# Output projection of a hybrid diffusion layer: rounded tokens kept over both column halves, the two contraction halves in PSUM tiles of their own, squares summed by column half

## The chip, the cores and the metric

The kernel runs on one core of a Trainium2 chip. The metric is the device time of one execution in microseconds (us). Five engines work beside each other, each in its own program order: TensorE (PE; its weight loads are listed as PEld), VectorE (DVE), ScalarE (ACT), GpSimd (POOL) and SyncE (SP, which issues most DMAs). They wait for each other through semaphores.

## The reference, cut to what matters

One layer over 128 context tokens and 512 latent tokens, model width 1024. Attention and a gated convolution each give 512 columns per token; each half is RMS-normed on its own, both together go through one output projection, and a feed-forward block follows.

```
merged = concat([_rms(attn, attn_out_norm), _rms(y_conv, conv_out_norm)], axis=-1)   # 512 + 512
mix = merged @ w_out                                  # (tokens, 1024) @ (1024, 1024)
x  = x + g1 * mix
h2 = _rms(x, norm_ffn) * (1 + sc2) + sh2              # the mean of squares runs over all 1024 columns
gate, up = split(h2 @ w_gate_up)                      # DFF = 2816
x  = x + g2 * ((silu(gate) * up) @ w_down)
```

`_rms(v, g) = v * rsqrt(mean(v*v) + 1e-6) * g`. The inverse norms of the two halves, `rA` (attention) and `rB` (convolution), are numbers per token, so they can be applied after the matmul, to the product of each half.

## The kernel before, in words

Every float32 operand is split into a rounded part and a rest (`split`, L146: ACT writes the high part, DVE subtracts to get the low part), and a product is three matmuls (`mm3`, L150: high x high, high x low, low x high).

The output projection is the loop at L1037. It runs over two column halves `j` of `w_out` (512 columns each) and, in each, over five tiles of 128 tokens: the context tile first, then latent tiles 0 to 3 (`TORD`). For each tile the tokens are the stationary operand: four 128-row blocks of the attention half `of` and four of the convolution half `yf`. Both halves are split anew in each `j` (`mix_half`, L968), except for the attention half of the context tile, which was split earlier (`mix_ctx`). The products of the halves go to the two banks of one PSUM tile `ab`; 24 matmuls per tile. Then ACT writes `m = ab[1]*rB`, DVE adds `ab[0]*rA`, multiplies by the gate `g1`, and adds `m` to the residual `x2` (L1071 to L1075; GpSimd does the last two steps for the first two tiles of `j = 0`). In `j = 1` ACT squares all 1024 columns of `x2` with a sum (L1080), DVE scales it, GpSimd takes the power -1/2, and DVE writes the normed tile `x2n` (L1082). `h2_turn` transposes a tile's `x2n` on TensorE, always after the 24 matmuls of the next tile of `j = 1`.

The weights of the projection come in eight blocks `("o", j, kp)` of two 128-row chunks, through three buffers `wf`; ACT (L244) writes the high part `wh` and DVE (L245) the low part `wl` with the norm gains folded in. Beside that, in `j = 0`, DVE accumulates the second gate in `aacc` (`g2_step`, L986 and L988, from four loads that go through the same three buffers).

Behind the projection the normed tokens are put, as high and low parts, into quarters: `B11`, `B21` for token columns 0 to 319 (LO), `B12`, `B22` for 320 to 639 (HI); `B12` is a buffer of the tag `gT`. Four differences `T1` to `T4` of the quarters follow (`b_sums`; its scratch is `tr`). The first two feed-forward blocks, f = 0 and 1 (`plain`, L1102), multiply by the quarters, first LO of both, then HI of both, 48 matmuls each. From f = 2 on, seven products by sums and differences of weight blocks are used (`op_load`: `S1` to `S4` are built in `sx`), in the order A11, S1, S2, A12, S3, A22, S4; S2 accumulates in the PSUM tile of A11, so it waits until ACT has copied that tile to `p1` (L1129).

TensorE's order is written out by hand (`manual_schedule` for PE, L467). On DVE, ACT, GpSimd and SP a scheduler puts the program into a fixed order at build time, after priorities that `early(n)` raises; at run time every engine keeps to that order. `BHD` names the quarters whose high part DVE writes instead of ACT.

Of the kernel before, what the change touches and what calls it, by code (L numbers as in the profile page):

```python
# [9 lines left out]
F32 = mybir.dt.float32  # L10
F32R = mybir.dt.float32r
AF = mybir.ActivationFunctionType
ALU = mybir.AluOpType
AX = mybir.AxisListType

P = 128
D = 1024
KD = D // P
NL = 4
NT = 5  # L20
TOK = NT * P
CTX = 4
# [8 lines left out]
EPS = 1e-6  # L31
# [30 lines left out]
H2E = [0, 0, 0, 2, 0]  # L62
PX = 2
SPO = 0
BHD = ("B21", "B22")
TL = 1
G2N = 0
PT = 2
# [1 line left out]
PHB = 2  # L70
XP = [50, 400]
BP = 300
AWB = 2
AO = 6
SOON = 150
# [12 lines left out]
def build(ctx, tc, x_prompt, x_sample, c, cache_k, cache_v, c_ctx, norm_mix, norm_ffn, w_ada, b_ada,  # L88
# [3 lines left out]
    act, dve, pool, pe, sp = nc.scalar, nc.vector, nc.gpsimd, nc.tensor, nc.sync  # L92
# [4 lines left out]
    def open_pool(name, side, names):  # L97
        g = tc.tile_pool(name=name, bufs=1, side=side, reuse_waits="tile")
        pools[name] = (g, g.__enter__())
        for n in names.split():  # L100
            where[n] = name

    def open_psum(name, bufs):
        g = tc.tile_pool(name=name, bufs=1, space=bass.MemoryType.PSUM, reuse_waits="tile")
        pools["psum"] = (g, g.__enter__())
        pbufs.clear()
        pbufs.update(bufs)
# [8 lines left out]
    def T(tag, shape, dt=F32, bufs=1):  # L116
        seq[0] += 1
        return pools[where.get(tag, "A")][1].tile(list(shape), dt, tag=tag, bufs=bufs, name=f"{tag}_{seq[0]}")
# [15 lines left out]
    def PS2():  # L134
        return PB((P, 2, 512), tag="s")
# [7 lines left out]
    def early(n):  # L143
        return tc.high_priority(n)

    def split(hi, lo, src):  # L146
        act.activation(hi, src, AF.Copy)  # L147
        dve.tensor_tensor(lo, src, f32(hi), ALU.subtract)  # L148

    def mm3(out, lh, ll, rh, rl, start, stop, more=False):  # L150
        pe.matmul(out, lh, rh, start=start, stop=False, skip_group_check=more)  # L151
        pe.matmul(out, lh, rl, start=False, stop=False, skip_group_check=more)  # L152
        pe.matmul(out, ll, rh, start=False, stop=stop, skip_group_check=more)  # L153
# [141 lines left out]
    for gi, grp in enumerate(GROUPS):  # L295
# [5 lines left out]
        for j in range(2):  # L301
            for i0 in range(0, len(grp), 2):
                n = len(grp[i0:i0 + 2])
# [450 lines left out]
    rB = [None] * NT  # L754
# [176 lines left out]
    close_pool("B1")  # L931
    close_pool("H")
    close_pool("psum")
    open_psum("pp3", {"t": 2, "c": 2, "s": 2})
    for x in PPO:
        for _ in range(1):
            kept[x] = [PS2() if x == "s" else PB(tag=x)]
    open_pool("X", "left", "x2 x2n g2 sx")
    open_pool("GT", "left", "gT")
    open_pool("Y1", "left", "B11 B21")  # L940
    open_pool("D", "right", "mix mH mL aacc bb")
    phase[0] = 2


# [20 lines left out]
                else:  # L965
                    act.activation(dst, tp[:, i], AF.Identity, bias=b, scale=a)

    def mix_half(src):  # L968
        mh = T("mH", (P, 4, P), F32R, 4)
        ml = T("mL", (P, 4, P), F32R, 4)  # L970
        split(mh, ml, src)
        return mh, ml

    g2 = [T("g2", (P, D), F32, 2) for _ in range(2)]
    g2acc = [None, None]
# [61 lines left out]
    for j in range(2):  # L1037
        cols = slice(j * 512, (j + 1) * 512)
        for n, t in enumerate(TORD):
            cc = 1 if t == CTX else 0  # L1040
            c0 = t * P + (2 if t == CTX else 0)
            ms = [mix_ctx if t == CTX else mix_half(of[t]), mix_half(yf[:, :, c0:c0 + P])]
            ab = PS2()
            for half in range(2):
                for p in range(4):
                    wh, wl = W(("o", j, 2 * half + p // 2))
                    mm3(ab[:, half], ms[half][0][:, p], ms[half][1][:, p], wh[:, p % 2], wl[:, p % 2],
                        p == 0, p == 3)
                if j == 0 and CRP == f"{n}{'me'[half]}":
                    next(ada_gen, None)  # L1050
                    conv_rms()
            if j == 1 and n:
                h2_turn(TORD[n - 1])
                with early(BP):
                    if n == 2:
                        b_plain("B11 B21", slice(0, 256))
                    if n == 3:
                        b_plain("B11 B21", slice(256, HALF))
            if j == 0 and n == 1:
                att_rms(NL - 1)  # L1060
                act.activation(warm, rA[NL - 1], AF.Silu)
            if j == 0 and G2N <= n < 4 + G2N:
                g2_step(0, n - G2N)
            if j == 1 and n == 0:
                g2_out(0)
            if j == 0:
                x2[t] = T("x2", (P, D), F32, NT)
                sp.dma_start(x2[t], x_dram[t])
            with early(XP[j]):
                m = T("mix", (P, 512), F32, 2)  # L1070
                act.activation(m, ab[:, 1], AF.Copy, scale=rB[t])  # L1071
                dve.scalar_tensor_tensor(m, ab[:, 0], rA[t], m, ALU.mult, ALU.add)
                e = pool if j == 0 and n < PX else dve
                e.tensor_tensor(m, m, g1[cc][:, cols], ALU.mult)
                e.tensor_tensor(x2[t][:, cols], m, x2[t][:, cols], ALU.add)  # L1075
            if j == 1:
                with early(XP[j]):
                    x2n[t] = T("x2n", (P, D), F32, 1)
                    ss = T("ss", (P, 1), F32, 6)
                    act.activation(x2n[t], x2[t], AF.Square, accum_out=ss)  # L1080
                    r = rstd_of(ss, 1, 1.0 / D)
                    dve.tensor_scalar_mul(x2n[t], x2[t], r)  # L1082


# [211 lines left out]
```

## Time and profile before

| | |
|---|---|
| median of 3 runs | 761.24 us (761.2 to 762.45) |
| the profiled execution | 762.03 us, of which its span (first to last instruction) is 760.3 us |
| granted TensorE clock, mean | 0.995 |
| DMA | 84.52 MB in 102349 packets, mean 111 GB/s |
| chain that ended last | PE 80%, DVE 9%, ACT 3%, DMA 3% of the span |

All durations further down come from the profiled execution; times are counted from its first instruction. In rows of the timeline the first number is the start, the second the duration, and a bracket at the end names idle time of that engine ahead of the row and what ended it. Consecutive instructions of one engine overlap a little, so the distance of two starts is what one of them costs in a row of many.

### The profile page before, as it was taken

The page shows a single profiled execution, that of the slowest core. Times are in us where ns is not written, and L with a number is a line of the kernel's source. Part 1 is how long each engine was busy: PE and PEld are TensorE (multiplying, and loading weights), DVE is VectorE, ACT ScalarE, POOL GpSimd, SP SyncE. Part 2 cuts the span into 40 slices and gives each one's busy share as a digit, 9 for nine tenths or more (in the row PEclk, how much of TensorE's full clock was granted, in tenths as well). Part 3 has the DMA queues.
Part 4 walks back from the last instruction along what each step waited for, and adds up shares of the span by engine and source line. Part 5 has one row for each costly group of instructions (what it writes and reads, how often), then busy time and mean ns, then how long its engine had stood idle before and what let it go on. Part 6 is the DMA issues. An engine that isn't in the chain of part 4 may idle for free.

```text
span 760.3 us, 11889 instructions
## 1 busy us (share of the span) xinstructions
PE 738.2 (97%) x4580; PEld 663.4 (87%) x4580; DVE 559.1 (74%) x1009; ACT 373.6 (49%) x713; POOL 48.7 (6%) x77
## 2 busy tenths in 40 slices
PE   4999999999999999999999999999999999999997
PEld 3778988989999887799998789998889998899986
DVE  5556987676567799799879678875578866788653
ACT  5355776666555445865552135552125541255410
POOL 2104201011010130000000000000000000000000
PEclk9899999999999999999999999999999999999999
DMA  9994133423423453031325223223113132232312
GB/s 291 289 258 138 43 111 110 155 91 106 159 91 117 156 199 112 1 111 56 112 90 176 85 66 98 81 90 111 52 56 111 57 111 80 60 87 81 112 55 84
DMA packets 102349, 84.52 MB, mean 111 GB/s; under 512 B 4526, under 2 KB 82674, under 8 KB 102292
## 3 DMA queue, kind: packets, MB, share of 16 engines
q1 hardware_dynamic: 100980, 83.39, 36.1%
q8 instruction: 36, 0.59, 0.3%
q10 hardware_dynamic: 1056, 0.26, 0.2%
q14 instruction: 21, 0.17, 0.1%
q0 software_dynamic: 256, 0.11, 0.1%
HBM read 79.68 MB, written 2.75 MB: 108 GB/s over the span
## 4 chain that ended last, share of the span: by engine, by line
PE 80%; DVE 9%; ACT 3%; DMA 3%; issue 2%; SPq 1%; POOL 1%; POOLq 0%; DVEq 0%; ACTq 0%
PE pf L151 17%; PE pf L152 17%; PE pf L153 17%; PE pc L674 3%; PE pc L675 3%; PE pc L676 3%; PE ps L788 2%; PE po L831 2%; PE pt L814 2%; PE ps L151 2%; DMA af<-in_w_ada_dram 2%; PE pc L376 2%; PE ps L152 2%; PE ps L153 2%; POOL rs L161 1%
## 5 line engine op out<-in xcount | busy, mean ns | idle before, releaser
L147 ACT ACTIVATE wh<-wf 128x1024 fp32r<-128x1024 f32 (+1 forms) x76 | 64.2, 844 | 92.7 <-PE pf L153 63.1
L151 PE MATMUL pf<-wh,gT 128*128 128x512 f32 (+1 forms) x225 | 88.1, 391 | 0.0
L152 PE MATMUL pf<-wl,gT 128*128 128x512 f32 (+1 forms) x225 | 87.7, 390 | 0.0
L153 PE MATMUL pf<-wh,gT 128*128 128x512 f32 (+1 forms) x225 | 87.6, 390 | 0.0
L148 DVE TENSOR_TENSOR wl<-wf,wh 128x1024 fp32r<-128x1024 f32 (+1 forms) x42 | 49.3, 1174 | 28.1 <-ACT wh L147 25.2
L674 PE MATMUL pc<-hH,wh 128*128 128x320 f32 x192 | 61.1, 318 | 0.0
L676 PE MATMUL pc<-hH,wl 128*128 128x320 f32 x192 | 59.4, 309 | 0.0
L675 PE MATMUL pc<-hL,wh 128*128 128x320 f32 x192 | 59.3, 309 | 0.0
L151 PEld LDWEIGHTS pf<-wh,gT 128*128 128x128 f32 x225 | 42.2, 188 | 9.9 <-ACT wh L147 0.2
L152 PEld LDWEIGHTS pf<-wl,gT 128*128 128x128 f32 x225 | 42.2, 188 | 9.9 <-issue 0.2
L153 PEld LDWEIGHTS pf<-wh,gT 128*128 128x128 f32 x225 | 42.2, 188 | 9.8
L151 PE MATMUL pf<-T,wh 128*128 128x320 f32 x160 | 49.3, 308 | 1.5 <-ACT p L1129 1.5
L151 PE MATMUL pf<-T,wl 128*128 128x320 f32 x160 | 49.2, 308 | 0.0
L152 PE MATMUL pf<-T,wl 128*128 128x320 f32 x160 | 49.2, 308 | 0.0
L153 PE MATMUL pf<-T,wl 128*128 128x320 f32 x160 | 49.2, 308 | 0.0
L152 PE MATMUL pf<-T,wh 128*128 128x320 f32 x160 | 49.2, 308 | 0.0
L153 PE MATMUL pf<-T,wh 128*128 128x320 f32 x160 | 49.2, 307 | 0.0
L151 PE MATMUL pf<-B,wl 128*128 128x320 f32 x152 | 46.9, 308 | 0.0
L152 PE MATMUL pf<-B,wl 128*128 128x320 f32 x152 | 46.8, 308 | 0.0
L153 PE MATMUL pf<-B,wl 128*128 128x320 f32 x152 | 46.8, 308 | 0.0
L1208 DVE TENSOR_TENSOR dm<-pf,g 128x512 f32<-128x512 f32 (+1 forms) x41 | 27.7, 675 | 23.1 <-PE pf L153 23.1
L147 ACT ACTIVATE wl<-wf 128x512 fp32r<-128x512 f32 x34 | 21.4, 630 | 43.5 <-PE pf L152 36.8
(282 smaller groups left out, 2055.7 us busy)
## 6 DMA issues: line engine op xcount, KB each, us to landing
wf<-in_w_gate_up_dram SPq DMA_DIRECT2D x44, 512.0 KB, 4.0
aw<-in_w_ada_dram SPq DMA_DIRECT2D x24, 512.0 KB, 4.8
wf<-in_w_down_dram SPq DMA_DIRECT2D x20, 512.0 KB, 3.4
wf<-in_w_in_dram SPq DMA_DIRECT2D x18, 512.0 KB, 5.7
af<-in_w_ada_dram SPq DMA_DIRECT2D x32, 256.0 KB, 5.8
x<-in_x_sample_dram SPq DMA_DIRECT2D x8, 512.0 KB, 5.2
wf<-in_w_out_dram SPq DMA_DIRECT2D x8, 512.0 KB, 4.7
wf<-in_w_ada_dram SPq DMA_DIRECT2D x8, 512.0 KB, 3.8
```

The lines of the kernel that those rows point to most:

```text
L147: act.activation(hi, src, AF.Copy)
L148: dve.tensor_tensor(lo, src, f32(hi), ALU.subtract)
L151: pe.matmul(out, lh, rh, start=start, stop=False, skip_group_check=more)
L152: pe.matmul(out, lh, rl, start=False, stop=False, skip_group_check=more)
L153: pe.matmul(out, ll, rh, start=False, stop=stop, skip_group_check=more)
L376: pe.matmul(out[CG * g:CG * (g + 1)], cp[:, k], w, start=(k < 4), stop=(k >= KD - 4), skip_group_check=True)
L674: pe.matmul(acc, wh[:, k], hH[k][:, c0:c0 + n], start=(k == 0), stop=False)
L675: pe.matmul(acc, wh[:, k], hL[k][:, c0:c0 + n], start=False, stop=False)
L676: pe.matmul(acc, wl[:, k], hH[k][:, c0:c0 + n], start=False, stop=(k == KD - 1))
L788: pe.matmul(s2[:, g, :320], q, kk[:, v, P + g * 320:P + (g + 1) * 320], start=(i == 0), stop=(i == 1))
L814: pe.transpose(tp[:, i, h], u[3][h][:, kt * P:(kt + 1) * P], ident)
L1208: dve.tensor_tensor(dm, ps[:, :n], g2[cc][:, oc], ALU.mult)
```

## The change

The changed kernel splits each token tile once, in `j = 0`, and keeps the result for `j = 1` (tag `mx`, eight buffers; the last tile's convolution half borrows a buffer of `sx`); the splits get a priority of their own (`MXP`). The attention and convolution products go to two PSUM tiles of one bank each (tag `h`, four of them, in place of two tiles of two banks). In `j = 0` ACT now evicts the attention half and DVE adds the convolution half. In `j = 1` DVE alone evicts: each half is scaled by its norm and by `g1` in one instruction and added to `x2`, the attention half with a priority (`AP0`) of its own. The squares are summed over 512 columns in each `j`: `ms0` keeps the first half's mean plus epsilon, and `j = 1` adds to it. The high part of `B22` moves from DVE to ACT (`BHD`).

```
-BHD = ("B21", "B22")
+BHD = ("B21",)
+AP0 = 60
+MXP = [300, 200, 0, 0, 0]
...
-    open_psum("pp3", {"t": 2, "c": 2, "s": 2})
+    open_psum("pp3", {"t": 2, "c": 2, "h": 4})
...
-    open_pool("D", "right", "mix mH mL aacc bb")
+    open_pool("D", "right", "mix mx aacc bb")
...
-    def mix_half(src):
-        mh = T("mH", (P, 4, P), F32R, 4)
-        ml = T("mL", (P, 4, P), F32R, 4)
-        split(mh, ml, src)
-        return mh, ml
+    def mix_half(src, tag="mx"):
+        w = T(tag, (P, 2, 4, P), F32R, 8 if tag == "mx" else 2)
+        split(w[:, 0], w[:, 1], src)
+        return w[:, 0], w[:, 1]
+
+    mixed, ms0 = {}, {}
...
-            ms = [mix_ctx if t == CTX else mix_half(of[t]), mix_half(yf[:, :, c0:c0 + P])]
-            ab = PS2()
+            if j == 0:
+                with early(MXP[n]):
+                    mixed[t] = [mix_ctx if t == CTX else mix_half(of[t]),
+                                mix_half(yf[:, :, c0:c0 + P], "sx" if t == NL - 1 else "mx")]
+            ms = mixed[t]
+            ab = [PB(tag="h") for _ in range(2)]
...
-                act.activation(m, ab[:, 1], AF.Copy, scale=rB[t])
-                dve.scalar_tensor_tensor(m, ab[:, 0], rA[t], m, ALU.mult, ALU.add)
-                e = pool if j == 0 and n < PX else dve
-                e.tensor_tensor(m, m, g1[cc][:, cols], ALU.mult)
-                e.tensor_tensor(x2[t][:, cols], m, x2[t][:, cols], ALU.add)
-            if j == 1:
-                with early(XP[j]):
+                if j == 0:
+                    act.activation(m, ab[0], AF.Copy, scale=rA[t])
+                    dve.scalar_tensor_tensor(m, ab[1], rB[t], m, ALU.mult, ALU.add)
+                    e = pool if n < PX else dve
+                    e.tensor_tensor(m, m, g1[cc][:, cols], ALU.mult)
+                    e.tensor_tensor(x2[t][:, cols], m, x2[t][:, cols], ALU.add)
+                else:
+                    with early(AP0):
+                        dve.scalar_tensor_tensor(m, ab[0], rA[t], g1[cc][:, cols], ALU.mult, ALU.mult)
+                        dve.tensor_tensor(x2[t][:, cols], m, x2[t][:, cols], ALU.add)
+                    m = T("mix", (P, 512), F32, 2)
+                    dve.scalar_tensor_tensor(m, ab[1], rB[t], g1[cc][:, cols], ALU.mult, ALU.mult)
+                    dve.tensor_tensor(x2[t][:, cols], m, x2[t][:, cols], ALU.add)
+            ss = T("ss", (P, 1), F32, 6)
+            with early(XP[j]):
+                act.activation(m, x2[t][:, cols], AF.Square, accum_out=ss)
+                if j == 0:
+                    ms0[t] = T("ms0", (P, 1), F32, NT)
+                    dve.tensor_scalar(ms0[t], ss, 1.0 / D, EPS, ALU.mult, ALU.add)
+                else:
+                    q = T("ms", (P, 1), F32, 4)
+                    dve.tensor_scalar(q, ss, 1.0 / D, ms0[t], ALU.mult, ALU.add)
+                    r = T("rs", (P, 1), F32, 6)
+                    pool.tensor_tensor(r, q, neghalf[:, :1], ALU.pow)
                     x2n[t] = T("x2n", (P, D), F32, 1)
-                    ss = T("ss", (P, 1), F32, 6)
-                    act.activation(x2n[t], x2[t], AF.Square, accum_out=ss)
-                    r = rstd_of(ss, 1, 1.0 / D)
                     dve.tensor_scalar_mul(x2n[t], x2[t], r)
```

TensorE's order is the same in both kernels. On DVE and ACT the scheduler's order changes from the first `mx` split to the end of f = 2, then it is the same again. Three places matter below. A row is a line, an operation, out<-in with the number of the buffer's use, and a size; "x2" is two of them. Lines of the changed kernel are 2 to 23 higher.

Place 1, DVE at the end of `j = 0`, before: `mix_3537` is latent tile 2, and `wl_3345`, `wl_3353`, `wl_3361` are the low parts of the first three weight blocks of `j = 1`.

```order
L1072 SCALAR_TENSOR_TENSOR mix_3537<-ps_3503,rA_2874,mix_3537 128x512
L1074 TENSOR_TENSOR mix_3537<-mix_3537,g_166_697 128x512
L245 SCALAR_TENSOR_TENSOR wl_3345<-wf_3342,vec_143,wh_3344 128x512 x2
L1075 TENSOR_TENSOR x_835_3535<-mix_3537,x_835_3535 128x512
L245 SCALAR_TENSOR_TENSOR wl_3353<-wf_3350,vec_143,wh_3352 128x512 x2
L245 SCALAR_TENSOR_TENSOR wl_3361<-wf_3358,vec_143,wh_3360 128x512 x2
```

DVE there in the changed kernel, from the end of the `aacc` sums on: `mix_3496` is latent tile 1, `mix_3546` latent tile 2, `ms_823`, `ms_832` are `ms0` of latent tiles 0 and 1, `wl_3428` is the fourth weight block and `mix_3642` the attention half of the context tile in `j = 1`.

```order
L1098 TENSOR_SCALAR ms_823_3453<-ss_3451 128x1
L1080 SCALAR_TENSOR_TENSOR mix_3496<-ph_3462,rB_3338,mix_3496 128x512
L1082 TENSOR_TENSOR mix_3496<-mix_3496,g_166_697 128x512
L1083 TENSOR_TENSOR x_829_3494<-mix_3496,x_829_3494 128x512
L1098 TENSOR_SCALAR ms_832_3503<-ss_3501 128x1
L1080 SCALAR_TENSOR_TENSOR mix_3546<-ph_3512,rB_3338,mix_3546 128x512
L1082 TENSOR_TENSOR mix_3546<-mix_3546,g_166_697 128x512
L1083 TENSOR_TENSOR x_838_3544<-mix_3546,x_838_3544 128x512
L247 SCALAR_TENSOR_TENSOR wl_3345<-wf_3342,vec_143,wh_3344 128x512 x2
```

ACT at the same place in the changed kernel: the squares (with `ss`) stand between the evictions (`mix`) and the high weight parts (`wh`).

```order
L1095 ACTIVATE mix_3446,ss_3451<-x_820_3444 128x512
L1079 ACTIVATE mix_3496<-ph_3461,rA_2492 128x512
L1095 ACTIVATE mix_3496,ss_3501<-x_829_3494 128x512
L1079 ACTIVATE mix_3546<-ph_3511,rA_2874 128x512
L246 ACTIVATE wh_3344<-wf_3342,vec_143 128x512 x2
L1095 ACTIVATE mix_3546,ss_3551<-x_838_3544 128x512
```

The residual add of latent tile 2 and the two `ms0` stand ahead of `wl_3345` now, in a row in which DVE and ACT each use what the other wrote last; the token splits that stood here are gone. DVE a little further on, in the changed kernel:

```order
L1080 SCALAR_TENSOR_TENSOR mix_3589<-ph_3562,rB_3338,mix_3589 128x512
L1082 TENSOR_TENSOR mix_3589<-mix_3589,g_166_697 128x512
L247 SCALAR_TENSOR_TENSOR wl_3428<-wf_3425,vec_143,wh_3427 128x512
L1086 SCALAR_TENSOR_TENSOR mix_3642<-ph_3598,rA_1508,g_167_698 128x512
L247 SCALAR_TENSOR_TENSOR wl_3428<-wf_3425,vec_143,wh_3427 128x512
```

An eviction now stands between the two halves of the fourth weight block's low part.

Place 2, DVE behind the last `x2n` (latent tile 3), before: the `gT` row of 128x4x128 is the low part of the last 128 token columns of `B12`.

```order
L1082 TENSOR_SCALAR x2n_3900<-x_842_3575,rs_3905 128x1024
L148 TENSOR_TENSOR wl_3948<-wf_3596,wl_3948 128x512
L148 TENSOR_TENSOR wh_3951<-wf_3604,wh_3951 128x512
L148 TENSOR_TENSOR wl_3954<-wf_3604,wl_3954 128x512
L1019 TENSOR_TENSOR gT_3920<-gT_3283,gT_3920 128x4x192
L1019 TENSOR_TENSOR B_910_3923<-gT_3284,B_910_3923 128x4x192
L1019 TENSOR_TENSOR T_912_3928<-tr_3926,T_912_3928 128x4x192
L1019 TENSOR_TENSOR T_914_3933<-tr_3931,T_914_3933 128x4x192
L964 TENSOR_SCALAR gT_3283<-pt_4009,modA_31_146,modB_33_148 128x128 x2
L964 TENSOR_SCALAR gT_3284<-pt_4018,modA_31_146,modB_33_148 128x128 x2
L1019 TENSOR_TENSOR gT_3920<-gT_3283,gT_3920 128x4x128
```

In the changed kernel `x2n` is followed by two 128x512 low parts of weights, the 128x4x192 rows of `gT_3910` (B12) and `B_908` (B22), one more low part, and then by these rows:

```order
L150 TENSOR_TENSOR wl_3944<-wf_3617,wl_3944 128x512
L1035 TENSOR_TENSOR tr_3916<-gT_3283 128x768
L205 TENSOR_TENSOR sx_4030<-wf_4025 128x512
L1035 TENSOR_TENSOR tr_3921<-gT_3284,tr_3916 128x768
L1022 TENSOR_TENSOR T_910_3918<-tr_3916,T_910_3918 128x4x192
L1035 TENSOR_TENSOR tr_3926<-gT_3284,gT_3283 128x768
L1022 TENSOR_TENSOR T_912_3923<-tr_3921,T_912_3923 128x4x192
L1035 TENSOR_TENSOR tr_3931<-gT_3284,tr_3921 128x768
L1022 TENSOR_TENSOR T_914_3928<-tr_3926,T_914_3928 128x4x192
L966 TENSOR_SCALAR gT_3283<-pt_3999,modA_31_146,modB_33_148 128x128 x2
L966 TENSOR_SCALAR gT_3284<-pt_4008,modA_31_146,modB_33_148 128x128 x2
L1022 TENSOR_TENSOR gT_3910<-gT_3283,gT_3910 128x4x128
```

The differences `tr` and the third `T`, which stood ahead of `x2n` or behind `gT`, stand between them now, with one more weight row and an `sx`.

Place 3, DVE in f = 1 and 2, before: `cu_4112` is the last HI product of f = 1, `wl_4049` the low part of A12 of f = 2, `sx_4264` the first sum for f = 3, from the buffer `wf_4243`.

```order
L148 TENSOR_TENSOR wl_4049<-wf_4033,wl_4049 128x512
L203 TENSOR_TENSOR sx_4040<-wf_4033,sx_4040 128x512
L1019 TENSOR_TENSOR T_916_3938<-tr_4123,T_916_3938 128x4x128
L148 TENSOR_TENSOR wh_4065<-sx_4040,wh_4065 128x512
L1032 TENSOR_TENSOR tr_4127<-gT_3284,tr_4119 128x4x128
L1112 TENSOR_TENSOR cu_4006<-pf_4132,cg_4005 128x320
L148 TENSOR_TENSOR wl_4080<-wf_4035,wl_4080 128x512
L1019 TENSOR_TENSOR T_918_3943<-tr_4127,T_918_3943 128x4x128
L148 TENSOR_TENSOR gT_4183<-cu_4006,gT_4183 128x640
L203 TENSOR_TENSOR sx_4264<-wf_4243 128x512
L148 TENSOR_TENSOR wh_4096<-sx_4040,wh_4096 128x512
L1112 TENSOR_TENSOR cu_4112<-pf_4187,cg_4111 128x320
```

In the changed kernel the same things are `wl_4039` (A12 of f = 2, from `wf_4023`), `sx_4254` (from `wf_4233`, a load into the buffer that `wf_4023` leaves) and `cu_4102`:

```order
L205 TENSOR_TENSOR sx_4030<-wf_4023,wf_4025 128x512
L150 TENSOR_TENSOR wh_4036<-sx_4030,wh_4036 128x512
L205 TENSOR_TENSOR sx_4030<-wf_4023,sx_4030 128x512
L1135 TENSOR_TENSOR cu_3996<-pf_4122,cg_3995 128x320
L150 TENSOR_TENSOR wl_4039<-wf_4023,wl_4039 128x512
L150 TENSOR_TENSOR gT_4173<-cu_3996,gT_4173 128x640
L150 TENSOR_TENSOR wh_4055<-sx_4030,wh_4055 128x512
L150 TENSOR_TENSOR wl_4070<-wf_4025,wl_4070 128x512
L205 TENSOR_TENSOR sx_4254<-wf_4233 128x512
L205 TENSOR_TENSOR sx_4254<-sx_4254,wf_4231 128x512
L150 TENSOR_TENSOR wh_4086<-sx_4030,wh_4086 128x512
L1135 TENSOR_TENSOR cu_4102<-pf_4177,cg_4101 128x320
```

The last reader of the old buffer (before the `sx` row that is second, now `wl_4039`) stands eight rows ahead of the first reader of the new load before, and four rows ahead now.

More of the change, by code (lines that the diff above doesn't have):

```diff
@@ L1046, in build @@
                     wh, wl = W(("o", j, 2 * half + p // 2))
[L1047 removed]
+                    mm3(ab[half], ms[half][0][:, p], ms[half][1][:, p], wh[:, p % 2], wl[:, p % 2],
                         p == 0, p == 3)
```

## The prediction

> **What bounds the kernel now.** First the page: busy time by engine, then the waits of TensorE (who waited for whom: total, times, longest) in the stretch that the change touches, 255 to 360 us.
>
> ```profile
> PE 738.2 (97%) x4580; PEld 663.4 (87%) x4580; DVE 559.1 (74%) x1009; ACT 373.6 (49%) x713; POOL 48.7 (6%) x77
> ...
> PE pf L151 <- ACT p L1129: 1.5, 1, 1.5
> PE pt L958 <- DVE x2n L1082: 1.4, 3, 0.5
> PE ps L152 <- DVE wl L245: 0.2, 1, 0.2
> ```
>
> TensorE is busy for 97% of the span, its order and its matmuls stay as they are, so the change is worth what it removes from or adds to TensorE's few waits. Three kinds are listed, 3.1 us in all. What feeds them shows in busy time by stretch (length; PE, PEld, DVE, ACT, POOL; granted clock, DMA share, GB/s):
>
> ```profile
> 258.00:290.00 32.00, 31.88 (x150) 25.91 (x149) 30.70 (x47) 14.66 (x25) 9.19 (x6) 1.00 0.52 182
> 290.00:321.00 31.00, 29.92 (x136) 22.98 (x136) 24.36 (x41) 21.97 (x48) 2.04 (x4) 1.00 0.18 51
> 335.00:345.00 10.00, 10.00 (x70) 10.00 (x69) 9.88 (x19) 3.83 (x7) 0.00 (x0) 1.00 0.09 26
> ```
>
> VectorE is full in the first column half (30.70 of 32) and in the first feed-forward blocks (9.88 of 10), and has room only in the second column half. So VectorE's order decides what TensorE waits for. The clock is 1.00 in all three and drops out.
>
> **Gain at the start and at the turns: -0.4 and -1.7 us.** TensorE's timeline:
>
> ```profile
> 258.92 0.40 PE L152 MATMUL ps<-wl,mH 128*128 128x512 f32 x1
> 259.44 0.50 PE L153 MATMUL ps<-wh,mL 128*128 128x512 f32 x1
> 259.77 0.40 PE L151 MATMUL ps<-wh,mH 128*128 128x512 f32 x1
> ...
> 300.19 0.40 PE L152 MATMUL ps<-wl,mH 128*128 128x512 f32 x1
> 300.42 0.39 PE L153 MATMUL ps<-wh,mL 128*128 128x512 f32 x1
> 301.20 1.09 PE L958 MATMUL pt<-ident,x2n 128*128 128x128 f32 x8 [0.38 <-DVE x2n L1082]
> ```
>
> Projection matmuls start 0.235 apart. The first low part `mL` came late: 0.52 and 0.33 instead of 0.235 twice, 0.38 lost; the changed order puts that split three places further forward, so this goes. The turn shown has 0.38 idle and costs 0.78 - 0.24 = 0.54, so 0.16 more than its idle time; the three turns of the table, 1.4 idle, cost 1.4 + 3 x 0.16 = 1.9. The chain from a tile's last matmul to `x2n`:
>
> ```profile
> L1071 ACT ACTIVATE mix<-ps,rB x10: 669/672/712, 266.0 to 321.8; 128x512 f32<-128x512 f32 x10
> L1072 DVE SCALAR_TENSOR_TENSOR mix<-ps,rA,mix x10: 737/746/750, 266.8 to 323.7; 128x512 f32<-128x512 f32 x10
> L1075 DVE TENSOR_TENSOR x<-mix,x x8: 682/691/692, 282.2 to 325.2; 128x512 f32<-128x512 f32 x8
> ...
> L1080 ACT ACTIVATE x2n<-x x5: 1042/1085/1092, 298.4 to 326.0; 128x1024 f32<-128x1024 f32 x5
> L1080 ACT ACTIVATION_READ_ACCUMULATOR x2n<-x x5: 186/228/232, 299.4 to 327.0; 128x1 f32 x5
> L1082 DVE TENSOR_SCALAR x2n<-x,rs x5: 752/754/755, 300.4 to 329.2; 128x1024 f32<-128x1024 f32 x5
> ...
> L161 POOL TENSOR_TENSOR rs<-ms,neghalf x5: 548/549/1193, 299.8 to 327.9; 128x1 f32<-128x1 f32 x5
> ```
>
> Before: 0.67 + 0.75 + 2 x 0.69 + 1.09 + 0.23 + about 0.15 (`ms`) + 0.55 + 0.75 = 5.6, against 24 x 0.235 = 5.6 us of matmuls that cover it: no slack. Now: 0.75 + 0.69, a square of 512, 0.15 + 0.55 + 0.75. That square with its sum is not in the trace; it lies between half the 1024 form (0.54) and the whole with its read (1.31), and I take 0.72, half plus most of the read. Sum 3.6: two us of slack at the first two turns. At the third the `B11` and `B21` work stands between, and I get `x2n` 0.15 late. So 1.7 of the 1.9 goes. The five evictions added on DVE (5 x 0.75) lie in the stretch with room, in place of nine low splits of 0.68.
>
> **Loss at the start of the second column half: +1.9 us.** VectorE and neighbours there:
>
> ```profile
> 280.72 0.74 DVE L1072 SCALAR_TENSOR_TENSOR mix<-ps,rA,mix 128x512 f32<-128x512 f32 x1
> 282.22 0.69 DVE L1075 TENSOR_TENSOR x<-mix,x 128x512 f32<-128x512 f32 x1
> 282.83 0.69 DVE L148 TENSOR_TENSOR mL<-y,mH 128x512 fp32r<-128x512 f32 x1
> 285.42 1.41 DVE L245 SCALAR_TENSOR_TENSOR wl<-wf,vec,wh 128x512 fp32r<-128x512 f32 x2
> ...
> 267.65 1.67 POOL L1074 TENSOR_TENSOR mix<-mix,g 128x512 f32<-128x512 f32 x1 [1.65 <-DVE mix L1072]
> 268.08 1.78 DVE L148 TENSOR_TENSOR mL<-of,mH 128x512 fp32r<-128x512 f32 x1
> ...
> 286.86 0.38 SPq L221 DMA_DIRECT2D wf<-in_w_out_dram  x1
> 290.18 1.34 ACT L244 ACTIVATE wh<-wf,vec 128x512 fp32r<-128x512 f32 x2 [1.51 <-DMA wf<-in_w_out_dram]
> 287.26 0.40 PE L151 MATMUL ps<-wh,m 128*128 128x512 f32 x1
> 293.33 1.88 PE L996 MATMUL pt<-aacc,ones 128*128 128x512 f32 x4
> ```
>
> I walked the new orders of DVE, ACT, POOL and SP from 254 us with such distances of starts: 0.66 for a gain or `aacc` instruction, 0.60 for a 512 split, 1.50 for evict and gate and 0.61 for the add. A DVE row that meets a POOL multiply costs 1.1 more (1.78 against 0.68), four times in both kernels. All nine token splits are done by 269; in return `rB` and the `aacc` sums slide back, and the last sum ends near 280.7 (before 280.2). From there the order of place 1 binds: DVE waits for ACT's eviction of latent 1 (280.9, behind a square that waits for POOL), evict, gate, add (283.0), waits for the square (283.9), `ms0`, waits for ACT's eviction of latent 2 (284.5), another 2.11, and only then `wl_3345` at 286.6, before 285.42. Its halves end at 287.35 and 288.0. TensorE reaches them at 286.9 (287.26 less 0.38) and loses 0.35. The fourth block's load waits for that buffer: issued at 288.0 instead of 286.86, so with the 3.32 from there to ACT's start, ACT works on it at 291.3, its two high parts end at 292.0 and 292.6, the low parts, with an eviction of 0.66 between them, at 292.85 and 294.2. TensorE is there at 291.4 and waits about 0.65, 0.7 and 0.6. That is 2.3 us of waits; the old kernel lost (293.33 - 287.26) - 24 x 0.235 = 0.43 here. So +1.9. If DVE came through 1.2 us sooner, nothing would be lost.
>
> **Loss at the second half of f = 0: +2.3 us; at f = 2: none.** By these sums TensorE starts the feed-forward at -0.4 + 1.9 - 1.7 = -0.2. Rows there:
>
> ```profile
> 329.84 0.69 DVE L148 TENSOR_TENSOR wl<-wf,wl 128x512 fp32r<-128x512 f32 x1
> 330.44 0.69 DVE L148 TENSOR_TENSOR wh<-wf,wh 128x512 fp32r<-128x512 f32 x1
> 331.64 0.95 DVE L1019 TENSOR_TENSOR gT<-gT,gT 128x768 fp32r<-128x768 f32 x1
> 332.51 0.95 DVE L1019 TENSOR_TENSOR B<-gT,B 128x768 fp32r<-128x768 f32 x1
> 335.12 1.36 DVE L964 TENSOR_SCALAR gT<-pt,modA,modB 128x128 f32<-128x128 f32 x4
> 336.60 0.69 DVE L1019 TENSOR_TENSOR gT<-gT,gT 128x512 fp32r<-128x512 f32 x1
> ...
> 338.01 0.31 PE L151 MATMUL pf<-gT,wh 128*128 128x320 f32 x1
> 357.23 0.42 PE L151 MATMUL pf<-T,wh 128*128 128x320 f32 x1 [1.46 <-ACT p L1129]
> ...
> 355.60 0.48 DVE L1112 TENSOR_TENSOR cu<-pf,cg 128x320 f32<-128x320 f32 x1
> ...
> wf<-in_w_gate_up_dram SPq DMA_DIRECT2D x44, 512.0 KB, 4.0
> ```
>
> Before, between the last `x2n` and the low part of `B12` stand 3 x 0.60 + 4 x 0.87 + 1.36 = 6.6 us, and `gT` starts at 336.60: 0.7 us before TensorE reads it at 338.16. Now (place 2) stand 5 x 0.60 + 9 x 0.87 + 1.36 = 12.2. The last `x2n` comes sooner, because its tile's eviction no longer queues behind three weight rows: my walk ends it at 327.2 (row before: next start 329.84). So `gT` starts at 339.4 and ends at 340.1. TensorE, there at 337.8, waits some 2.3 us.
>
> From there TensorE needs, as before (338.01 to 357.23 less the 1.46), 17.8 us to S2: 357.9. DVE needs, from the start of `gT`, 0.87 for the fourth `T`, 16 rows of 0.60 and three `cu` of 0.40, 11.7 us, to the A12 row (place 3), whose end at 351.8 frees the `wf` buffer. Only then the load is issued; it takes 4.0 (DMA row of the page), so `sx_4254` starts near 355.8. Three rows of 0.60 and `cu` follow (358.1), and from `cu`'s end to TensorE's start it is 1.15 as before (356.08 to 357.23): TensorE goes on at 359.3, having waited 1.4 where it waited 1.5. So DVE's smaller load wins no time before `cu_4102`, since that stands behind the new load. `B22`'s high parts, moved to ACT, are missing from these DVE counts, and ACT has room for them (3.83 of 10 in the stretch above).
>
> **Sum.** -0.4 - 1.7 + 1.9 + 2.3 + 0.0 = **+2.1 us**. From the end of f = 2 on the orders agree and TensorE has no wait as long, so a shift there stays. Against the profiled execution (762.03, 1.7 around its span) that is 764.1; the median shown is 761.24, hence **763.3**. The bounds: the new low split of the start not earlier, +0.4; start of the half between no wait at all (-2.3) and a second late load row (+1.0); `gT` between in time (-2.3) and one row of 0.87 more; the load between 3.3 (the w_out row) and 5 us, -0.7 and +1.0.
>
> [...]
>
> **Rivals.** (1) *The gains hold and DVE keeps up: faster.* Mechanism: DVE's unbroken queue behind tile latent 3 is shorter than I add, so that B12's low part is ready before 337.8. It decides there: 2.3 us of DVE rows less. Then -0.4 - 0.4 - 1.7 and S2's 1.5 go: 757.2. For it: nine splits less on DVE. Against: 9 x 0.87 cannot shrink, and windows show DVE at 9.88 of 10. Chance 0.10. (2) *One of the two losses fails to come: no change.* Without the late weights (ACT's square and evictions overlapping better than in my walk) the sum is 2.1 - 2.3 = -0.2, 761.0; without a late load at f = 2 it is 2.1 - 1.45 = +0.65, 761.9. The price of each lies in places where my times meet within 1 us. Chance 0.28. (3) *GpSimd is shut out:* its power for `rA` and the add behind it come between back-to-back `aacc` rows; the row of `rs` above shows it held up by 0.64 at most (1193 against 549), which is one DVE row. If it waited for all three, ACT's square, which waits for it, holds up all of place 1 by 1.1: 764.4. [...] Chance 0.07. (4) That the change does not do what it says: the built order shows nine splits less, so not weighed.
>
> **How the numbers follow.** Forecast 0.55, rivals 0.10, 0.28, 0.07. About 0.2% (1.5 us) is what a measurement of this kernel can tell from no change. Forecast and (3) lie over +1.5: slower 0.62; (2) is the same: 0.28; (1) faster: 0.10. The range leaves out (1) and the far end of the bounds above: 760.3 to 765.2.
>
> **What would show it.** Right: no wait of the turns for `x2n` (one of 0.2 at most); TensorE waiting for `wl` and `wh` of the output weights for 2 us right at `j = 1`; a wait of about 2.3 for `gT` at the first product with `B12`; again 1.5 for `p`, behind a DVE wait for a gate/up load. Wrong, if TensorE runs through 338 us without a stall, or if `wl_3345` ends before TensorE has finished `j = 0`.

## The result, and the profile after

The changed kernel takes 765.16 us (median of 6 runs, 764.62 to 767.5) beside 761.56 us of the kernel before on the same chip: ratio 1.0055, 95% interval 1.0037 to 1.0073, or +4.2 us (the ratio is of the means; the medians differ by 3.6). In a second measurement it was 765.61 beside 762.15, ratio 1.0046 [1.0028, 1.0064]. The forecast had +2.1 us: the right side, and half the size, at the upper end of its range (765.2).

The waits of TensorE in the profiled execution of the changed kernel (764.62 us, span 762.8), 250 to 372 us; who waited for whom: total, times, longest:

```profile
PE pf L153 <- ACT gT L1021: 3.1, 1, 3.1
PE ph L154 <- DVE wl L247: 0.6, 2, 0.4
PE ph L153 <- ACT wh L246: 0.5, 1, 0.5
PE pf L154 <- DVE gT L1022: 0.3, 1, 0.3
```

The three turn waits for `x2n` are gone, the late output weights are there, and the wait for `p` of 1.5 us has dropped out of the list. The wait for `gT` (B12) is 3.4 us in two pieces instead of 2.3. Around it the busy time by stretch (length; PE, PEld, DVE, ACT, POOL; granted clock, DMA share, GB/s) shows something the forecast did not have:

```profile
336.00:340.00 4.00, 0.89 (x5) 0.49 (x4) 3.88 (x8) 3.65 (x8) 0.00 (x0) 1.00 0.00 0
340.00:344.00 4.00, 3.69 (x15) 3.60 (x15) 3.96 (x7) 1.13 (x3) 0.00 (x0) 0.57 0.00 0
344.00:348.00 4.00, 4.00 (x29) 4.00 (x28) 4.00 (x8) 2.86 (x6) 0.00 (x0) 1.00 0.00 0
```

After a stretch in which TensorE was busy for 0.89 of 4 us, the granted clock is 0.57 for one stretch, and only 15 matmuls pass in it where the next has 29.

The best way to read two traces with one order of matmuls is matmul by matmul. For the same matmul I take its start in a trace less its start in the trace of before; what this shift gains between two places is what the stretch between them cost. The places lie at 256, 261, 286, 297, 324, 348, 363 and 400 us of the trace of before. The two executions of before and after were already 1.45 us apart at the first place, where both programs are still the same; so the spans alone (760.3 and 762.8) would hide more than a third of the loss.

| us | start of projection | rest of j = 0 | start of j = 1 | turns | B12 (HI, f = 0) | S2 | f = 2 | sum |
|---|---|---|---|---|---|---|---|---|
| forecast | -0.4 | | +1.9 | -1.7 | +2.3 | 0.0 | 0 | +2.1 |
| changed kernel | -0.4 | 0.0 | +2.0 | -1.7 | +5.5 | -1.3 | 0.0 | +4.0 |
| the same, again (e9) | -0.4 | 0.0 | +1.9 | -1.7 | +5.5 | -0.8 | 0.0 | +4.4 |
| e1 first sum late | -0.4 | 0.0 | +1.9 | -1.8 | +4.1 | -1.7 | 0.0 | +2.1 |
| e2 differences late | -0.4 | 0.0 | +1.9 | -1.8 | 0.0 | +1.3 | 0.0 | +1.0 |
| e3 both first sums late | -0.4 | 0.0 | +1.9 | -1.8 | +4.1 | -1.7 | 0.0 | +2.1 |
| e4 full squares | -0.4 | 0.0 | +0.2 | -1.5 | +2.6 | -0.3 | 0.0 | +0.7 |
| e5 kept tokens only | -0.4 | +0.6 | -0.5 | -1.4 | +0.5 | 0.0 | 0.0 | -1.2 |
| e6 = e4 + e2 + copy | -0.4 | 0.0 | +0.2 | -1.5 | 0.0 | -0.1 | +1.2 | -0.6 |
| e7 = e2 + copy | -0.4 | 0.0 | +2.0 | -1.8 | +0.3 | +0.3 | +0.9 | +1.4 |
| e8 = e5 + copy | -0.4 | +0.6 | -0.5 | -1.4 | +0.5 | -1.7 | +0.8 | -2.1 |
| e10 = e8 + tiles | -0.4 | 0.0 | -0.5 | -1.4 | +0.5 | -1.7 | +0.6 | -2.8 |
| e11 = e10 + B22 on ACT | -0.4 | 0.0 | -0.5 | -1.4 | +0.6 | -1.7 | +0.5 | -2.9 |
| e12 B22 back on DVE | -0.4 | 0.0 | +2.2 | -1.7 | +5.4 | -1.5 | 0.0 | +3.9 |

Three of the five terms came as forecast. The other two are one story. VectorE of the changed kernel from the last `x2n` to `gT`, in part (start, duration; brackets: idle time ahead and what ended it), ScalarE's row for the high part of `gT`, and SyncE's loads there:

```profile
325.10 0.75 DVE L1105 TENSOR_SCALAR x2n<-x,rs 128x1024 f32<-128x1024 f32 x1 [0.44 <-POOL rs L1103]
...
329.31 0.68 DVE L150 TENSOR_TENSOR wl<-wf,wl 128x512 fp32r<-128x512 f32 x1
329.91 0.95 DVE L1035 TENSOR_TENSOR tr<-gT 128x768 f32<-128x768 f32 x1
332.36 0.69 DVE L205 TENSOR_TENSOR sx<-wf 128x512 f32<-128x512 f32 x1 [1.50 <-DMA wf<-in_w_gate_up_dram]
...
339.66 0.69 DVE L1022 TENSOR_TENSOR gT<-gT,gT 128x512 fp32r<-128x512 f32 x1
339.00 0.63 ACT L1021 ACTIVATE gT<-gT 128x512 fp32r<-128x512 f32 x1 [0.34 <-DVE gT L966]
327.13 3.26 SPq L223 DMA_DIRECT2D wf<-in_w_gate_up_dram  x2
```

`sx_4030`, the first weight sum of f = 2, waits 1.50 us for its load. It is the first of the two loads in the last row, issued at 327.13, when an earlier `wl` row (326.37 to 327.05) had read the old buffer; by the trace it landed at 332.33, 5.2 us after its issue, where the median of these loads is 3.9 in this trace. (The second, issued at 330.02, is for f = 3.) VectorE stands still for those 1.50 us with `gT` queued behind it: the four rows L966 that write `gT` in float32, and the low part at 339.66. The high part, on which TensorE's 3.11 us of waiting end below, is ScalarE's, and it too had waited for the last of VectorE's L966 rows. TensorE's side, the last product ahead of the stall and those behind it:

```profile
336.26 0.31 PE L155 MATMUL pf<-B,wl 128*128 128x320 f32 x1
339.68 0.41 PE L153 MATMUL pf<-gT,wh 128*128 128x320 f32 x1 [3.11 <-ACT gT L1021]
340.40 0.52 PE L154 MATMUL pf<-gT,wh 128*128 128x320 f32 x1 [0.31 <-DVE gT L1022]
340.72 0.47 PE L155 MATMUL pf<-gT,wh 128*128 128x320 f32 x1
340.99 0.47 PE L153 MATMUL pf<-gT,wh 128*128 128x320 f32 x1
...
343.92 0.34 PE L155 MATMUL pf<-B,wl 128*128 128x320 f32 x1
344.10 0.31 PE L153 MATMUL pf<-B,wl 128*128 128x320 f32 x1
344.25 0.30 PE L154 MATMUL pf<-B,wl 128*128 128x320 f32 x1
```

At 340.72 TensorE is 4.0 us behind (340.72 - 336.26 - 3 x 0.147). The 12 matmuls from there on start 0.267 apart instead of 0.147: another 1.45, together 5.5. And at S2, VectorE, ScalarE and TensorE:

```profile
356.22 0.69 DVE L205 TENSOR_TENSOR sx<-wf 128x512 f32<-128x512 f32 x1 [1.51 <-DMA wf<-in_w_gate_up_dram]
...
358.16 0.48 DVE L1135 TENSOR_TENSOR cu<-pf,cg 128x320 f32<-128x320 f32 x1
358.68 0.74 ACT L149 ACTIVATE gT<-cu 128x640 fp32r<-128x640 f32 x1 [1.87 <-DVE cu L1135]
359.32 0.42 ACT L1152 ACTIVATE p<-pf 128x320 f32<-128x320 f32 x1
359.35 0.31 PE L155 MATMUL pf<-T,wl 128*128 128x320 f32 x1
359.79 0.41 PE L153 MATMUL pf<-T,wh 128*128 128x320 f32 x1
```

The chain that was forecast stands there, row by row (load, `sx`, `cu`, `gT`'s high part, `p`), but TensorE arrives so late that it loses only 0.3 us to it.

### The profile page after: what moved, and what is told of

It reads as the page before. It is cut to its first block, busy times and chain, and to the rows that moved or that the text cites. A ratio compares the mean times of both kernels' runs of the same rounds, so it can differ in the third digit from the quotient of the medians.

```text
span 762.8 us, 11866 instructions
## 1 busy us (share of the span) xinstructions
PE 740.0 (97%) x4580; PEld 664.3 (87%) x4580; DVE 558.8 (73%) x1008; ACT 368.8 (48%) x711; POOL 48.9 (6%) x77
## 4 chain that ended last, share of the span: by engine, by line
PE 80%; DVE 9%; DMA 4%; issue 2%; ACT 2%; SPq 1%; POOL 1%; POOLq 0%; DVEq 0%; ACTq 0%
PE pf L153 17%; PE pf L154 17%; PE pf L155 17%; PE pc L676 3%; PE pc L677 3%; PE pc L678 3%; PE ps L790 2%; PE po L833 2%; PE pt L816 2%; PE pc L378 2%; DMA af<-in_w_ada_dram 2%; DMA wf<-in_w_gate_up_dram 1%; PE ps L153 1%; DVE aacc L991 1%; PE ph L154 1%
```

## The experiments

Two theories were open. A: what sets the end is the release of S2, that is VectorE's queue from the last `x2n` on; the stall at B12 lies ahead of it. B: the stall and the slow matmuls are the loss. Ratios below are to the kernel before, on the same chip. An edit that orders two rows is a copy of 128x1 that reads the one and is overwritten by the other.

**e1, e3: the first weight sums later.**

```
+    behind = {2: lambda: f32(B["B12"][4][:, 1, 0, HALF - 1:HALF])}   # e3 also: 3: lambda: last_cu[1][:, TOK - 1:TOK]
...
                 sums[f] = T("sx", (P, 2, 4, P), F32, 2)
+                if f in behind:
+                    dve.tensor_copy(sums[f][:, 0, 0, 0:1], behind[f]())
```

> The changed kernel, with one more 128x1 copy on VectorE that puts the first weight sum of f = 2 (which waited 1.5 us for its load, ahead of B12's low part) behind B12's low part. Theory A: what sets the end is the release of product S2 of f = 2, that is VectorE's queue from the last x2n to the fourth load; the stall at B12 and the slow matmuls behind it only come ahead of that release. Then the 1.5 us wait goes from VectorE's queue, gT starts about 1.3 us sooner (338.4 where it was 339.7), the stall shrinks from 4.0 to about 2.7 and the 1.5 us of slow matmuls go, but TensorE then waits about 2 us at S2 where it waited 0.3: in all -2.1 us, about 763.1 where the changed kernel has 765.2. Rival B: the stall and the slow matmuls themselves are the loss and S2 is no limit: -2.8 to -3.0 us, 762.3 or less, with no wait at S2.

> As the run with the first sum of f = 2 behind B12's low part, and the first sum of f = 3 (whose load is issued late) behind the last product of f = 1, by one more 128x1 copy. Theory A: no VectorE wait for a load stands between the last x2n and S2 any more. TensorE's stall at B12 is as in the first run, about 2.7 us, but it does not wait at S2: -2.8 us, near 762.4, that is 0.7 under the first run. Rival B: the same as the first run, since by it S2 was no limit there.

Measured: e1 763.88 us, ratio 1.0026 [1.0015, 1.0038]; e3 763.39, 1.0023 [1.0009, 1.0036]. By the traces both give back 1.9 us: to have the sum and its load wait out of the way of `gT` was worth that. But where A wanted a wait at S2 in e1 there is none, and e1 and e3 have the same shifts; between their times the intervals decide nothing. TensorE in e1:

```profile
338.40 0.31 PE L155 MATMUL pf<-B,wl 128*128 128x320 f32 x1
339.77 0.41 PE L153 MATMUL pf<-gT,wh 128*128 128x320 f32 x1 [1.07 <-ACT gT L1025]
341.15 0.41 PE L154 MATMUL pf<-gT,wh 128*128 128x320 f32 x1 [0.97 <-DVE gT L1026]
...
341.90 0.47 PE L155 MATMUL pf<-gT,wh 128*128 128x320 f32 x1
342.17 0.47 PE L153 MATMUL pf<-gT,wh 128*128 128x320 f32 x1
...
345.29 0.31 PE L153 MATMUL pf<-B,wl 128*128 128x320 f32 x1
```

The stall is down to 2.0 us of idle time, and the slow matmuls come all the same (341.90 to 345.29). They are what brings TensorE to S2 too late to wait there; A had left them out.

**e2: the first 192 columns of T1 to T4 behind B12's low part.**

```
-                b_sums(two[0])
                 for x in range(NPLAIN):
...
                             b_plain("B12 B22", two[1])
+                        b_sums(two[0], f32(B["B12"][4][:, 1, 0, HALF - 1:HALF]))
```

> The changed kernel, with the first 192 columns of all four differences T1 to T4 put behind B12's low part on VectorE (one more 128x1 copy orders them). Their 7 rows of 0.87 us no longer stand ahead of gT; the weight sum with its load wait still does, so gT starts near 335.3 and ends at 336.0, before TensorE's arrival at 336.4: no stall at B12 (0.3 at most), no slow matmuls. VectorE's work up to the last product of f = 1 is the same, so by theory A (VectorE's queue up to S2 sets the end) S2 comes at about 357.5 instead of 359.8 and TensorE waits about 3 us there: -2 to -2.5 us, near 763. Rival B (the stall is the loss): all 5.5 us come back, 759.7, and TensorE does not wait at S2.

Measured: 764.49 us, ratio 1.0039 [1.0024, 1.0053]; the profiled run is the fastest of its six (763.77). In its trace the stall and the slow matmuls are gone, all 5.5 us, and this stands in the list of waits and at S2:

```profile
PE pf L153 <- ACT p L1154: 2.7, 1, 2.7
```
```profile
357.31 0.48 DVE L1137 TENSOR_TENSOR cu<-pf,cg 128x320 f32<-128x320 f32 x1
357.82 0.74 ACT L149 ACTIVATE gT<-cu 128x640 fp32r<-128x640 f32 x1 [0.96 <-DVE cu L1137]
358.47 0.42 ACT L1154 ACTIVATE p<-pf 128x320 f32<-128x320 f32 x1
358.94 0.41 PE L153 MATMUL pf<-T,wh 128*128 128x320 f32 x1 [2.71 <-ACT p L1154]
```

By the trace that is A (a wait of about 3 us and -2 to -2.5 expected; 2.7 and -3.0 measured), and B, which wanted 759.7, falls: of 5.5 us taken away ahead of S2, 2.6 (1.3 + 1.3 in the table) come back as a wait there. So two limits lie close together, the stall with its slow matmuls and VectorE's queue up to `cu`. Counted in the time of the trace of before, S2 starts at 358.2 in e2 (358.94 - 0.74, by which e2 is late at the first place) and at 361.2 in the changed kernel (359.79 + 1.45): the release is 3.0 us sooner, and so is the end. Not all of that is the edit's aim. In the built order of e2 the first sum of f = 3 stands behind `cu` (358.31 against 357.31), while in the changed kernel it waits 1.51 us for its load ahead of `cu`; so VectorE's work up to `cu` was less, where the expectation had it the same. The times give e2 less than its trace, 0.5 to 1.2 us under the changed kernel: its other five runs had mean clocks down to 0.991 and were up to 2.8 us longer than the profiled one.

**e4: squares over all 1024 columns again.**

```
             with early(XP[j]):
-                act.activation(m, x2[t][:, cols], AF.Square, accum_out=ss)
-                if j == 0:
...
+                if j:
+                    x2n[t] = T("x2n", (P, D), F32, 1)
+                    act.activation(x2n[t], x2[t], AF.Square, accum_out=ss)
+                    r = rstd_of(ss, 1, 1.0 / D)
```

> The changed kernel with one part undone: squares over all 1024 columns in the second column half, as before, none in the first. Theory: the squares by column halves made the row of place 1, in which VectorE and ScalarE wait for each other, so undoing them takes the late weights away: TensorE's waits at the start of the second half go from 2.4 to about 0.6 (-1.8 us). The turns still have no wait, since the DVE evictions made that chain short enough (4.2 us with the full square against 5.6 of matmuls). The order behind x2n loses the weight sum with its load wait, so the stall at B12 goes from 4.0 to about 2.7 with no slow matmuls. In all -3.5 to -4 us against the changed kernel, near 761.5, the time of the kernel before. Rival: the half squares were needed for the turns (-1.75 us of gain): then waits of 0.3 to 0.5 us for x2n come back at three turns and the time is near 763.

Measured: 762.67 us, ratio 1.0009 [0.9999, 1.0019]. The waits:

```profile
PE pf L153 <- ACT gT L1021: 1.7, 1, 1.7
PE pf L153 <- ACT p L1146: 1.2, 1, 1.2
PE ph L154 <- DVE wl L247: 0.4, 1, 0.4
PE pt L960 <- DVE x2n L1099: 0.3, 1, 0.3
PE pf L154 <- DVE gT L1022: 0.3, 1, 0.3
```

As expected: the start of j = 1 costs 0.2 instead of 2.0, so the half squares made the late weights; the turns lose only 0.3 of their gain; the stall is 2.0 us and is followed by no slow matmuls. Of the parts that were tried alone the half squares cost the most, and they win next to nothing.

**e5: the kept tokens alone, in the kernel before.** The diff's lines on `mx`, `mixed` and `MXP`, nothing else.

> The kernel before, with one part of the change alone: the rounded tokens kept for the second column half. Theory: this part takes nine 512 splits (0.60 us each) off VectorE and adds none of the rows that lay ahead of B12's low part, so it cannot lose: the late low part at the start goes (-0.4), VectorE reaches the first weights of the second half sooner (-0.2 to -0.4), B12's low part keeps its 0.7 us of slack, and the wait of 1.5 us at S2 stays: about -0.7, 761.0 beside a 761.75 of the kernel before (ratio 0.998 to 1.000). Rival: the splits moved forward are what pushes everything else back on VectorE (the sums of the gate, the first weights), and the kernel is 1 to 2 us slower, like a good part of the change.

Measured: 761.75 us beside 761.69, ratio 1.0003 [0.9993, 1.0013]: no change by time. The trace has -1.2 over this part of the program:

```profile
PE pf L152 <- ACT p L1135: 1.5, 1, 1.5
PE pt L959 <- ACT T L1020: 0.4, 1, 0.4
PE ps L152 <- DVE mix L1078: 0.3, 1, 0.3
PE pt L959 <- DVE x2n L1088: 0.2, 1, 0.2
```

The turn waits are down to 0.2 with the old evictions and the old square. The twelve runs had mean clocks of 0.992 to 0.997, those of before 0.993 to 1.000, so their clock was lower; why, is open, and with it whether this part alone is worth 0 or 1 us.

**e6, e7, e8: the copy p1 ahead of f = 1's product on ScalarE**, with the edits named in the table.

```
             if toks is HI:
-            ff_out(f, cu)
+            if f == NPLAIN - 1:
+                held.append(cu)
+            else:
+                ff_out(f, cu)
...
+        if behind is not None:
+            act.activation(gT[f][0][:, 0:1], behind[:, 0:1], AF.Copy)
...
         st[f] = [b1, copy_of("p1", b1), cg, None, None, None, None]
+        if held:
+            ff_out(f - 1, held.pop(), st[f][1])
```

> The changed kernel with three edits together: full squares (as in the run of that name), the differences T1 to T4 behind B12's low part (as in the second run), and on ScalarE the copy p1 of A11's product ahead of the high part of f = 1's product, which waited for VectorE (one more 128x1 copy on ScalarE orders it). Theory A: no stall at B12 (2.6 us in the run with full squares) and p1 no longer waits for VectorE's last product of f = 1, so the wait at S2 is 0 to 1.2 us: -1.5 to -2.5 us against the run with full squares, 760.2 to 761.2, that is the time of the kernel before or up to 1.5 us under it. Rival B (the stall is the loss, S2 no limit): the same here, so this run does not tell them apart; it shows whether the losses found are all there is.

> The second run (differences behind B12's low part) with the copy p1 of A11's product moved ahead of the high part of f = 1's product on ScalarE. In the second run TensorE waited 2.7 us at S2 and ScalarE's copy stood behind a row that needs VectorE's last product of f = 1, at 357.3. If that chain is what holds S2, the copy now starts behind ScalarE's low-hanging weight row, about 1.6 us sooner, and the wait at S2 falls from 2.7 to about 1.1: 762.9 where the second run has 764.5. If instead the wait at S2 is for something else (the operand weights of S2 or T2), the time stays and TensorE waits for that.

> The kernel before with the tokens kept and the copy p1 ahead of the high part of f = 1's product on ScalarE. Theory: the kept tokens give 0.7 and the wait of 1.5 us at S2 goes, since that copy waited only for its place in ScalarE's order: -2.2 us in all, near 759.5, faster than both kernels. Rival: VectorE's rows for S1, S2 and A12 come too late as well, so that TensorE waits for them instead and 1 us or less is won.

Measured: e6 762.4 us, ratio 1.0004 [0.9991, 1.0016]; e7 762.84, 1.0018 [1.0005, 1.0030]; e8 759.62, 0.9977 [0.9964, 0.9991] (one of its twelve executions took 1853 us; the comparison leaves it out). In e7 the wait at S2 falls to 1.7, not 1.1, and 0.9 comes back in f = 2:

```profile
PE pf L153 <- ACT p L1161: 1.7, 1, 1.7
PE pf L153 <- DVE cu L1192: 0.7, 1, 0.7
```

So the copy's place was worth something, and VectorE's queue takes it back a few microseconds later: with the differences put behind `gT` it seems to have no slack. e6 had 760.2 to 761.2 expected and misses that by a microsecond. Its trace has 1.2 us of new loss in f = 2, 0.7 of it a wait for the same `cu`; the late weights, the turns and B12 cost it next to nothing, and it stands level with the kernel before. In e8, whose VectorE has not got the change's order, the copy gives the whole 1.7 at S2 and returns 0.8.

**e10, e11: two PSUM tiles on top of e8, then B22 on ScalarE; e12: the changed kernel with B22 back; e9: the changed kernel again.**

```
-    open_psum("pp3", {"t": 2, "c": 2, "s": 2})
+    open_psum("pp3", {"t": 2, "c": 2, "h": 4})        # e10, e11
...
-BHD = ("B21", "B22")
+BHD = ("B21",)                                        # e11; e12 is the other way round
```

> The changed kernel as it is, beside the kernel before, on this chip: how far its time and its stall at B12 repeat. If the slow matmuls behind the stall come from the stall, a profile of it again has them (15 or so matmuls of 0.267 us instead of 0.147), and all its runs have a lower mean clock than the best of the kernel before. If they were chance, this profile may lack them, and then S2 should show a wait of 1.5 to 2 us instead, with the same end (theory A). Time: +2.9 to +4.2 us against the kernel before, ratio 1.004 to 1.0055.

> The kernel before with kept tokens and the copy p1 first (the run of that name, 759.6), and the two PSUM tiles of one bank for the two halves in place of one of two banks, with the old evictions and squares. In the run without them TensorE lost 0.5 us in the first column half waiting for an eviction to free the PSUM tile; with a tile for each half that wait should go: -0.5 us, about 759.1 (ratio 0.997). Rival: the bank was not what it waited for, or the earlier matmuls only wait later: no change.

> The same, and the high part of B22 on ScalarE instead of VectorE, as in the change. VectorE has three rows less (about 0.3 to 0.35 us each) between the last x2n and S2; TensorE had no wait of more than 0.4 us left there, so 0 to -0.4 us. If VectorE's queue still holds products of f = 2 back (0.3 us at one of them), up to 0.5.

> The changed kernel with one part undone: the high part of B22 back on VectorE. Three rows (0.3 to 0.6 us each) come back to VectorE, one of 128x4x192 ahead of gT and one of 128x4x128 behind it, while one T row of 0.87 goes behind. By theory A (VectorE's queue up to S2 sets the end) the time rises by what is added up to S2, 0.7 to 1.0 us: 766. If only the stall at B12 counts, the two exchanges ahead of gT cancel within 0.5 and the time stays.

Measured: e9 as told above, with the stall and the slow matmuls again (+5.5 at B12 in both traces). e10: 758.49 us, ratio **0.9951** [0.9937, 0.9964], the fastest of all; its waits here:

```profile
PE pt L959 <- ACT T L1020: 0.4, 1, 0.4
PE pf L152 <- DVE cu L1173: 0.3, 1, 0.3
PE pt L959 <- DVE x2n L1088: 0.2, 1, 0.2
```

The wait for `mix` of j = 0 is gone, as expected. e11: 759.85, 0.9964 [0.9950, 0.9977], no difference from e10. e12: 764.78, 1.0033 [1.0020, 1.0045]: A wanted 0.7 to 1.0 us more than the changed kernel, and there is no loss; in its trace S2 has no wait, so here the stall was the higher limit. B22's place is worth nothing that can be measured in either setting.

## Why the prediction was right or wrong

**Start, -0.4:** right, -0.4.

**Turns, -1.7:** the size is right, the reason is not, so the size is in part luck. The prediction had the chain from a tile's last matmul to `x2n` as the cause ("5.6 us of matmuls that cover it: no slack"). e5 keeps that chain and still wins 1.4 by leaving out the token splits of j = 1, each of which is a row on ScalarE and one on VectorE. Which of the two queues made the waits, and whether the shorter chain alone would have taken them away, no run separates. The rest of the change adds 0.3 to 0.4.

**Start of the second half, +1.9:** right with its mechanism (+2.0). Less the 1.45 us by which the executions differ, `wl_3345` starts at 286.58 (forecast 286.6) and the fourth block's load is issued at 288.0 (forecast 288.0):

```profile
281.68 0.63 ACT L1095 ACTIVATE mix<-x 128x512 f32<-128x512 f32 x1 [2.27 <-DVE x L1083]
283.01 0.75 DVE L1080 SCALAR_TENSOR_TENSOR mix<-ph,rB,mix 128x512 f32<-128x512 f32 x1 [0.42 <-ACT mix L1079]
285.13 1.41 DVE L247 SCALAR_TENSOR_TENSOR wl<-wf,vec,wh 128x512 fp32r<-128x512 f32 x2
286.57 0.38 SPq L223 DMA_DIRECT2D wf<-in_w_out_dram  x1
```

ScalarE stands idle for 2.27 us ahead of a square that needs VectorE's add, with the next high weight part behind it. e4 takes the squares away and 1.8 of the 2.0 with them.

**B12, +2.3:** here is the step that failed: "Now (place 2) stand 5 x 0.60 + 9 x 0.87 + 1.36 = 12.2." One of the five rows of 0.60 was `sx_4030`, the first reader of a new load. At place 3 the prediction followed such a row to its load's issue; at place 2 it counted it as a row, with a wait of nothing. The wait was 1.5 us. Followed in the same way, with the 4.0 us that the prediction had for such a load, it would have come to 0.3 only (327.13 + 4.0 = 331.13, against 330.86 at which VectorE got to the row); the other 1.2 is that this load took 5.2, beside another that was issued at 324.72 and landed at 329.45. The rest of the sum held: from `x2n`'s end, 325.85, 12.2 and the 1.5 of that wait give 339.6, measured 339.66. With it TensorE is 4.0 us late. The further 1.45 of slow matmuls no term had at all: "The clock is 1.00 in all three and drops out" held for the trace of before, and behind the longer stall the clock was 0.57 for one stretch. e1 shows the worth of the sum's place ahead of `gT`: 1.9 us of the end. (The slack of `gT` before, "0.7 us", is 0.87 by the prediction's own rows, 338.16 - 336.60 - 0.69; nothing hangs on it.)

**S2, 0.0:** -1.3, by the same error. The release of S2 came 1.9 us later than forecast (359.79 + 1.45 = 361.2 against 359.3) and TensorE 3.2 us later than the sum had it, so most of the wait was spent before it got there. The net error, 4.0 - 2.1 = 1.9, is this release. The slow matmuls seem not to have cost anything of their own in the changed kernel: without them TensorE would have waited at S2 that much longer. That is argued from the rows; no run had the same stall without them.

The rivals of the forecast did not come. GpSimd was not shut out (its power for `rA` takes 1.00 us, before 0.99), and no loss failed to come; the price of one was too low.

## What to carry to other kernels

A row that is the first reader of a load is not only its duration (here 0.69 us behind a wait of 1.50): follow it to the row that frees the buffer, to the issue and to the landing, at every place where the order moves, not only where a wait stood before, and allow for a load that takes longer than the median (5.2 us here, beside another load, where the prediction had 4.0). Taking a stall away can show the next limit behind it (2.6 of the 5.5 us came back in e2), so add up by place, matmul by matmul, before calling a stall the price. And try the parts of a change alone: here keeping the split tokens, with the two PSUM tiles and one copy moved forward, is 3.7 us faster (0.9951), while the half squares that came with them cost 3.3 us by the traces (4.0 against 0.7 in e4).

## What the hardware showed

TensorE's granted clock drops to half for stretches of 3.41 us (0.50 from 340.56 to 343.97 us in the changed kernel), and in before for one of twice that, 18.51 to 25.33 us. Leaving out the last microseconds of the program, before has only this one and the changed kernel has two, the other from 19.70 to 23.11; their starts are 320.86 us, 94 times 3.413, apart. In e1 rows of slow matmuls begin at 75.57 and at 341.90 us, 78.0 times 3.413 apart; the waits in the 5 us ahead of the first are 0.23 and 0.69. At B12 slow matmuls, 0.267 apart, followed in all five profiles in which TensorE idled for 2.0 us (e1, e3) to over 3 us (the changed kernel twice, e12) and not in e4, also with 2.0 us, where they stay 0.147 apart; in e2, 2.7 us of idle at S2 had none behind it. e1's two stretches around it; the second begins a little ahead of the first slow row:

```profile
338.18:341.59 3.41, 1.38 (x8) 0.89 (x7) 3.41 (x8) 2.16 (x4) 0.00 (x0) 1.00 0.00 0
341.59:345.00 3.41, 3.41 (x15) 3.41 (x15) 3.41 (x9) 1.63 (x3) 0.00 (x0) 0.53 0.00 0
```

TensorE had 1.38 us of work in the 3.41 us ahead of the low clock here, and 0.57 in the 3.41 us ahead of it in the changed kernel (337.15 to 340.56). The two stretches of 4 us over which e4's stall lies had 3.26 and 2.69, and the clock stayed at 1.00. The waits alone do not decide it everywhere: at the place where e1 had waits of 0.23 and 0.69 us and slow matmuls from 75.57 on, before had waits of 0.27 and 0.69, 2.32 us of work in 3.40 (72.10 to 75.50), and a clock of 1.00 behind them. So a stall with the same 2.0 us of idle time cost 4.1 at B12 in e1 and 2.6 in e4; what lowered the clock in the one and not in the other, no run shows. Single runs of one kernel spread over more than 3 us (before: 760.3 to 764.2, with mean clocks of 0.993 to 1.000), and the longer ones tend to have the lower clock; that such stretches make the spread is likely, but no run shows it by itself.
